# Three fused layers on one core: a recast second mixer, weight slots of twice the size, gate sums on VectorE

## The chip, the cores and the metric

One core of a Trainium2 chip runs one program: TensorE (PE), VectorE (DVE), ScalarE (ACT), GpSimdE (POOL) and SyncE (SP), each with its own instruction stream, joined by semaphores. The metric is the device time of one execution in microseconds, as the median of several. Everything is fp32; one fp32 matmul shows in the trace as two instructions, a transpose by matmul as one.

## The reference

A sequence of 256 tokens of width 1024 goes through two blocks. The first has two layers, each a mixer and an expert-choice mixture of experts (16 experts, 32 tokens each, width 1024); the second has one layer with a four-part mixer and a top-2 mixture of 16 experts of width 512. Each half layer is modulated by shift, scale and gate vectors, which are a vector times a large weight ("ada"). Shortened:

```python
cond = silu(c)
for l in range(2):                                   # first block
    shift, scale, gate = adaln(cond, ada_w[l, 0], ada_b[l, 0])        # 1024 x 3072
    h = rms_norm(x, mix_norm_g[l]) * (1 + scale) + shift
    y = fourier_conv_mixer(h) if l % 2 == 0 else windowed_attention(h)
    x = x + gate * y
    shift, scale, gate = adaln(cond, ada_w[l, 1], ada_b[l, 1])
    h = rms_norm(x, ffn_norm_g[l]) * (1 + scale) + shift
    x = x + gate * ec_moe(h)
x = rms_norm(x, final_norm_g)
# second block: ada_w_2 gives six vectors, for x and for the context ctx
hl, hc = modulated(rmsnorm(x)), modulated(rmsnorm(ctx))
u = hl @ w_in                                        # split into four parts of 256 columns each for:
a = diff_attention(...)          # 4 heads, 2 x 32 columns: softmax(q0 k0) - lam * softmax(q1 k1), then a norm per head
b = neighbourhood_attention(...) # 4 heads of 64, bias from a table
p = pool_mix(...); y = hyena_mix(...)                # y: two long convolutions by DFT matmuls
x = x + g1 * (concat(a, b, p, y) @ w_out)
x = x + g2 * moe(modulated(rmsnorm(x)))              # softmax router, best group of 4, top 2 in it
return rmsnorm(x, final_g)
```

## The kernel before, in words

All weights come from HBM once, in the order of a hand-written list (`order`), through a ring of `RING` = 14 slots of 1 MB in SBUF. `Stream.pump` issues the next transfer on SP's queue as soon as a slot is free; a slot is free when its user calls `st.done`. A transfer is [128 partitions x 8 KB]. The order is: constants and layer 0's `ada00`, `fc`, `ada01`, `fo`, then layer 0's 16 experts (three weights of 4 MB each), layer 1's attention weights and `ada`, its experts, the second block's `wi`, `ada20`, constants, `ada21`, `wo` (`w_out`), and its experts (w1, w3, w2 of 2 MB each).

`ada_steps` makes the vectors. "s" is the shift and scale half (16 pieces of 1024 columns), "g" the gate (8). With a letter in `ON_V`, VectorE adds the weight's rows, scaled by `cond`, into one tile (`add_rows`: L490 and L492, 128x1024 each), and TensorE only sums over partitions (L497); without it TensorE does all of the sums (L512, L555). These steps are fillers: the program calls `fill(n)` where an engine would wait. `weave` takes steps of several generators in turn, so that attention, projections (L1325, L1337), hyena, pooling and fillers stand between each other.

An expert-choice layer (`moe_ec`) first finds the norm of x, scales rows (`scale_rows`: L648 on VectorE, L649 on ScalarE), transposes (`plain_t`, L681), gets logits (L957, L963) and a softmax, picks each expert's tokens, gathers them by one-hot matmuls (L989) and runs the experts (L1052). Weighted rows go back by L1093, and in the last group x, its sum of squares and, after layer 1, the product with the final gain and its squares follow for each of four quarters (L1094, L614, L1099).

The second mixer (L1379 and on) norms twice, transposes (L659), projects (L1395, L1337, L1325), turns q and k (L1373) and then weaves. Attention A goes in 8 steps of one head: two score matmuls of 32 rows (L1436), reductions (L1442), exp (L1447), combination with lambda (L1452), four turns (L1419) and their copy (L1421), values (L1423, 4 matmuls of 64 columns). Its output is then normed and transposed again (`after_a`, L1373 on `oa`), and so is attention B's (L1373 on `va`). `wo` is L697. The last experts take tokens by top 2: `sc` are the softmaxed logits, L1689 to L1700 pick for one row block after the other, `keys` and `job` serve an extra run of a crowded expert, which is chosen at run time, `pair` gathers (L1743) for two experts, L1772 and L1797 are their matmuls.

On each engine instructions run in the order in which a scheduler of the framework put them; it starts from the order of the code and moves what is ready. The engines otherwise wait for semaphores alone.

## Time and profile before

| | |
|---|---|
| median of 3 runs | 1782.59 us (1780.39 to 1788.25) |
| profiled execution | 1785.29 us, of which the span is 1783.1 us |
| TensorE busy | 1421.8 us (80%), mean granted clock 0.857 |
| VectorE / ScalarE busy | 455.2 us (26%) / 242.9 us (14%) |
| moved by DMA | 635.93 MB, 357 GB/s on average |

The stages by TensorE's lines: mixer 0 to about 155 us, border of layer 0 to 184, its experts to 643, layer 1's attention to 775, its border and experts to 1272, the second mixer to 1468, the border to the last experts to 1498, these to 1763, the final norm and the output to the end. PE's share of busy time is an average over stages with different limits, so each stage is read by itself. The last 2 us between span and time lie around the span.

### The profile page before, as it was taken

The numbers are of one execution on the slowest core, as the hardware profiler recorded it, in microseconds if no ns is written. First come the engines' busy times: TensorE is split into PE (matmuls) and PEld (weight loads), VectorE is DVE, ScalarE is ACT, GpSimd is POOL, SyncE is SP. The second block draws the span as 40 slices with busy tenths as digits, with TensorE's granted clock in tenths as the row PEclk, the third lists the DMA queues.
The fourth block names the chain that finished last, engine by engine and source line by source line (L and its number), as shares of the span: only waits on it lengthen the run. The fifth ranks groups of instructions, "written<-read, shape, count | busy, mean of one in ns | idle before, by whom it ended". The sixth has DMA issues, their size and how long they took to land. (4 is left out here: it accounts for less than half of the span.)

```text
span 1783.1 us, 24944 instructions
## 1 busy us (share of the span) xinstructions
PE 1421.8 (80%) x10776; PEld 720.3 (40%) x10776; DVE 455.2 (26%) x1042; ACT 242.9 (14%) x556; POOL 10.7 (1%) x19
## 2 busy tenths in 40 slices
PE   6997877867666679987676776678799998999996
PEld 2444423323222234543232232235477745655453
DVE  2523212401010038541110100100333424333223
ACT  3021100100000012420200000000222312101012
POOL 0000000000000000000000000000000000000000
PEclk9997868878676689998787767868898998999998
DMA  9978899999999999289999999999931566999970
GB/s 375 421 310 325 346 420 421 420 421 421 420 422 421 420 410 408 101 354 420 421 420 421 421 420 421 421 421 420 409 107 51 206 242 239 421 421 415 392 297 25
DMA packets 89746, 635.93 MB, mean 357 GB/s; under 512 B 10944, under 2 KB 11072, under 8 KB 13344
## 3 DMA queue, kind: packets, MB, share of 16 engines
q1 hardware_dynamic: 87392, 630.67, 86.6%
q0 software_dynamic: 1952, 3.09, 0.5%
q8 instruction: 87, 1.43, 0.3%
q10 hardware_dynamic: 288, 0.52, 0.1%
q14 instruction: 27, 0.22, 0.0%
HBM read 633.25 MB, written 1.05 MB: 356 GB/s over the span
## 5 line engine op out<-in xcount | busy, mean ns | idle before, releaser
L1052 PE MATMUL b<-w,xg 128*32 128x256 f32 x4096 | 359.3, 493 | 172.6 <-DMA w<-in_moe_w_up_dram 99.8
L1052 PEld LDWEIGHTS b<-w,xg 128*32 128x32 f32 x4096 | 135.9, 132 | 392.7 <-DMA w<-in_moe_w_up_dram 150.2
L1052 PE MATMUL b<-w,hidT 128*32 128x256 f32 x2048 | 173.8, 476 | 71.5 <-DMA w<-in_moe_w_down_dram 55.3
L1072 DVE TENSOR_TENSOR hid<-b,sg 128x256 f32<-128x256 f32 x32 | 13.6, 425 | 499.0 <-PE b L1052 406.6
L1052 PEld LDWEIGHTS b<-w,hidT 128*32 128x32 f32 x2048 | 64.8, 130 | 166.6 <-DMA w<-in_moe_w_down_dram 95.3
L1772 PE MATMUL u<-w,xg 128*64 128x256 f32 x1088 | 128.0, 383 | 0.0
L1080 DVE SCALAR_TENSOR_TENSOR Y<-b,cc,gq 32x256 f32<-32x256 f32 x128 | 61.5, 481 | 224.2 <-PE b L1052 222.6
L1772 PEld LDWEIGHTS u<-w,xg 128*64 128x64 f32 x1088 | 78.2, 137 | 46.1 <-issue 10.3
L1797 PE MATMUL b<-w,hidT 128*64 128x512 f32 x272 | 65.8, 598 | 6.0 <-ACT hidT L1789 6.0
L1067 ACT ACTIVATE sg<-b 128x256 f32<-128x256 f32 x32 | 12.3, 383 | 424.7 <-PE b L1052 424.7
L697 PE MATMUL b<-w,n 128*128 128x512 f32 x128 | 56.0, 594 | 0.0
L1077 ACT COPY hidT<-b 128x256 f32<-128x256 f32 x32 | 11.9, 372 | 312.2 <-PE b L1075 312.2
L490 DVE SCALAR_TENSOR_TENSOR w<-w,cond 128x1024 f32<-128x1024 f32 x42 | 52.4, 1276 | 1.3 <-DMA w<-in_ada01s_dram 1.2
L1743 PE MATMUL b<-oh,n 128*128 128x128 f32 (+1 forms) x288 | 40.8, 301 | 3.5 <-DVE oh L1737 2.1
L1093 PE MATMUL b<-Y,gT 128*128 128x512 f32 x64 | 35.7, 702 | 9.5 <-DVE Y L1080 9.5
L1174 PE MATMUL b<-w,hT 128*128 128x512 f32 x96 | 43.1, 605 | 0.0
L1743 PEld LDWEIGHTS b<-oh,n 128*128 128x128 f32 x288 | 38.0, 212 | 11.3 <-issue 7.9
L822 PE MATMUL b<-w,hT 128*128 128x512 f32 x96 | 41.6, 593 | 1.1 <-DVE hT L671 1.1
L989 PE MATMUL b<-oh,n 128*128 128x128 f32 x256 | 39.9, 323 | 0.9 <-DVE oh L1032 0.9
L989 PEld LDWEIGHTS b<-oh,n 128*128 128x128 f32 x256 | 37.3, 233 | 7.2 <-issue 5.7
L1325 PE MATMUL b<-pe,w 128*128 128x256 f32 x160 | 38.6, 396 | 0.0
L1802 DVE TENSOR_TENSOR Y<-b,hkb 64x512 f32<-64x512 f32 x34 | 23.4, 688 | 53.6 <-PE b L1797 53.3
(439 smaller groups left out, 1383.9 us busy)
## 6 DMA issues: line engine op xcount, KB each, us to landing
w<-in_moe_w_gate_dram SPq DMA_DIRECT2D x128, 1024.0 KB, 19.8
w<-in_moe_w_up_dram SPq DMA_DIRECT2D x128, 1024.0 KB, 19.8
w<-in_moe_w_down_dram SPq DMA_DIRECT2D x128, 1024.0 KB, 19.8
w<-in_moe_w_dram SPq DMA_DIRECT2D x102, 1024.0 KB, 10.4
w<-in_wi_dram SPq DMA_DIRECT2D x10, 1024.0 KB, 19.8
w<-in_ada00s_dram SPq DMA_DIRECT2D x8, 1024.0 KB, 18.5
w<-in_ada01s_dram SPq DMA_DIRECT2D x8, 1024.0 KB, 20.6
w<-in_ada10s_dram SPq DMA_DIRECT2D x8, 1024.0 KB, 7.0
```

The source lines that it names most:

```text
L490: V.scalar_tensor_tensor(into[:, hs], w[:, hs], c, into[:, hs], op0=OP.mult, op1=OP.add)
L697: T.matmul(acc, mixT[:, kt, b * 128:(b + 1) * 128], w(kt)[:, h * 512:(h + 1) * 512], start=kt == first, stop=kt == last)
L822: T.matmul(p, hT[:, kt, b * 128:(b + 1) * 128], w(kt), start=kt == 0, stop=kt == 7)
L989: T.matmul(p[:, j * 128:(j + 1) * 128], n[:, b, dt * 128:(dt + 1) * 128], oh[:, b, g * 128:(g + 1) * 128], start=b == 0, stop=b == 1)
L1052: T.matmul(p[32 * q:32 * q + 32, :256], lhs(kt), w[:, k, q * 256:(q + 1) * 256], start=kt == 0, stop=kt == 7)
L1080: V.scalar_tensor_tensor(Y[32 * j:32 * j + 32, q * 256:(q + 1) * 256], pd[32 * q:32 * q + 32, :256], cc[32 * q:32 * q + 32, e:e + 1], gq[3 ...
L1093: T.matmul(p, gT[:, b * 128:(b + 1) * 128], Y[:, h * 512:(h + 1) * 512], start=True, stop=True)
L1174: T.matmul(p, hT[:, kt, b * 128:(b + 1) * 128], w(kt), start=kt == 0, stop=kt == 7)
L1325: T.matmul(p[:, j * 256:(j + 1) * 256], w(kt)[:, c0 + j * 128:c0 + (j + 1) * 128], h[:, kt], start=kt == 0, stop=kt == 7)
L1743: T.matmul(p[:, j * 128:j * 128 + m], n[:, b, dt * 128:(dt + 1) * 128], oh[:, b, :m], start=b == 0, stop=b == 1)
L1772: T.matmul(p[rows[h], :256], xg[:, kt, c], w[kt // 4][:, kt % 4, h * 256:(h + 1) * 256], start=kt == 0, stop=kt == 7)
L1797: T.matmul(pd[rows[h]], hidT[:, kt % 2, rows[kt // 2]], w[kt // 2][:, kt % 2, h * 512:(h + 1) * 512], start=kt == 0, stop=kt == 3)
```

## The change

It has seven parts. (1) `RING` becomes 7 with slots of 2 MB: the weights are laid out in HBM so that one transfer is [128 x 16 KB] and brings two of the former pieces; a slot frees when both are used, and a small constant takes a whole slot. (2) `ON_V`: the gates of (0,0) and (2,0) and all of (2,1) move to VectorE; in the second block these additions may stand only behind the last modulation or behind the first pair's one-hots (`queue_behind`). (3) The routers take x unnormalised and multiply the logits by r, and the rows are scaled after them; layer 1's last sums go to n first. (4) Both score copies of a step in layer 1's attention go to ScalarE. (5) The second mixer: one root of four columns, attention A in four steps of two heads with four score matmuls, values transposed in pairs of column tiles, no turns of the attentions' outputs, and reciprocals spread by matmuls. (6) In the last router both row blocks are picked by the same operations, and the first pair is gathered before the rest of the gate and the keys. (7) A job loads three transfers of 2 MB.

The core of the diff:

```diff
-ON_V = {(0, 0): "", (0, 1): "s", (1, 0): "g", (1, 1): "sg", (2, 0): "", (2, 1): ""}
-RING = 14
+ON_V = {(0, 0): "g", (0, 1): "s", (1, 0): "g", (1, 1): "sg", (2, 0): "g", (2, 1): "sg"}
+RING = 7
...
     def pump(self):
...
+            keys, shapes, ap = self.order[self.issued]
+            t = self.pool.tile([128, 2 * SLOT], F32, name="w")
+            self.nc.sync.dma_start(t[:, :ap.shape[1]], ap)
...
         def add_rows(kt, w, into):
+            with ExitStack() as behind:
+                if queue_behind:
+                    behind.enter_context(tc.issue_after(queue_behind[-1].ins))
+                add_rows_(kt, w, into)
...
-            scale_rows(n, x, rstd(ss))
-            fill(2)
             nT = [wk.tile([128, 8, 128], F32, name="xg", bufs=2) for _ in range(2)]
-            plain_t(nT, n)
+            plain_t(nT, x)
+            r = rstd(ss)
...
-            router(nT, rw, rbias, lg)
+            fill(2)
+            router(nT, rw, rbias, lg, r)
+            scale_rows(n, x, r)
...
+                        t = n[:, b, hs]
+                        V.tensor_tensor(t, x[:, b, hs], p, op=OP.add)
+                        A.activation(bank(), t, AF.Square, accum_out=ss[:, b, h:h + 1])
+                        V.tensor_tensor(x[:, b, hs], t, fg[:, h], op=OP.mult)
+                        sums(last, b, h, x)
...
-                    if u:
-                        A.copy(eT, p)
-                    else:
-                        V.tensor_copy(eT, p)
+                    A.copy(eT, p)
...
+            rs = inv_root(ms, 4)
+            r1, r2 = rs[:, 0:2], rs[:, 2:4]
             scale_rows(n, x, r2)
-            modulate(hT, turn(n), ada[2, 0])
+            queue_behind.append(modulate(hT, turn(n), ada[2, 0]))
             scale_rows(x, x, r1)
-            fill_until(lambda: ((2, 0), "g", 3) in st.freed)
...
+            def attend(po, es, vals, qb, j):
+
+                ets = [turned(e) for e in es]
+                at = j * 256 + qb * 128
                 for kb in range(4):
-                    T.matmul(po[:, h * 64:(h + 1) * 64], eT[:, kb * 128:(kb + 1) * 128], vals[:, kb, h * 64:(h + 1) * 64],
-                             start=kb == 0, stop=kb == 3)
+                    for u in range(2):
+                        h = 2 * j + u
+                        T.matmul(po[64 * u:64 * u + 64, at:at + 128], vals[:, kb, h * 64:(h + 1) * 64],
+                                 ets[u][:, kb * 128:(kb + 1) * 128], start=kb == 0, stop=kb == 3)
...
+                def scores(qb, j):
+                    pp = [bank() for _ in range(4)]
+                    for i in range(4):
+                        T.matmul(pp[i], qT[32 * i:32 * i + 32, j, qb * 128:(qb + 1) * 128], kT[32 * i:32 * i + 32, j], start=True, stop=True)
                     return pp
...
+            fill_until(lambda: (2, 0) in gqs and ((2, 0), "g", 0) in st.freed)
+            weave(hyena(), attention_b(), after_a(), chain(pooling(), filling(1, (2, 1))))
...
+            ts = {0: pair(0)}
+            queue_behind.append(ts[0]["last"])
+            fill(99)
```

What the scheduler makes of it, at three places. First TensorE in the second mixer, from the turns of q and k on. Before (L1373 turns, L1436 scores, L1325 projections, L1419 turns of the exponentials, L1423 values; x counts matmuls):

```order
L1373 MATMUL b<-cst,pe 128x128 x8
L1436 MATMUL b<-kT,qT 128x512 x4
L1325 MATMUL b<-pe,w 128x256 x8
L1419 MATMUL b<-cst,pe 128x128 x4
L1325 MATMUL b<-pe,w 128x256 x2
L1423 MATMUL b<-va,pe 128x64 x4
L1436 MATMUL b<-kT,qT 128x512 x2
L1325 MATMUL b<-pe,w 128x256 x6
L1419 MATMUL b<-cst,pe 128x128 x4
L1436 MATMUL b<-kT,qT 128x512
L1423 MATMUL b<-va,pe 128x64 x4
```

and after, where L1387, L1467, L1339 and L1351, L1432 and L1444 are the same in turn:

```order
L1387 MATMUL b<-cst,pe 128x128 x8
L1467 MATMUL b<-kT,qT 128x512 x4
L1339 MATMUL b<-pe,w 128x256 x16
L1351 MATMUL b<-w,pe 128x256 x16
L1432 MATMUL b<-cst,pe 128x128 x8
L1444 MATMUL b<-pe,va 64x128
L1467 MATMUL b<-kT,qT 128x512
L1444 MATMUL b<-pe,va 64x128 x7
L1467 MATMUL b<-kT,qT 128x512 x3
L1339 MATMUL b<-pe,w 128x256 x24
L1432 MATMUL b<-cst,pe 128x128 x8
L1467 MATMUL b<-kT,qT 128x512
```

The scores of the first step stand together, and those of the second stand as one among the eight value matmuls of the first step and three behind them; the third step begins in the same way. A step now has eight turns and eight value matmuls of 64x128.

Second TensorE at the border to the last experts. Before (L697 wo, L555 the gate's sums for `ada21g`, L681 transposes, L942 to L963 the router, L1702 the first rank sum):

```order
L697 MATMUL b<-w,n 128x512 x32
L555 MATMUL b<-w,cond 64x512 x6
L681 MATMUL b<-cst,n 128x128 x16
L942 MATMUL b<-vec,shsc_7693 128x16 x8
L957 MATMUL b<-xg,sg 32x128 x16
L555 MATMUL b<-w,cond 64x512
L963 MATMUL b<-cst,parts 128x16 x2
L555 MATMUL b<-w,cond 64x512 x9
L1702 MATMUL b<-one,cst 128x16
```

and after (L707 wo, L691 transposes, L952 to L973 the router, L1736 to L1740 the rank sums, L1777 and L1792 gather and scatter matrices, L1807 the first expert, L506 the gate's sum over partitions):

```order
L952 MATMUL b<-vec,shsc_7123 128x16 x8
L967 MATMUL b<-xg,sg 32x128 x16
L973 MATMUL b<-cst,parts 128x16 x2
L1736 MATMUL b<-one,cst 128x16
L1737 MATMUL b<-one,cst 128x16
L1738 MATMUL b<-one,cst 128x16
L1739 MATMUL b<-one,cst 128x16
L1740 MATMUL b<-one,cst 128x16
L1777 MATMUL b<-oh,n 128x128 x16
L1792 MATMUL b<-cst,ohg 128x128 x2
L1807 MATMUL u<-w,xg 64x256 x33
L506 MATMUL b<-w,cst 64x512 x2
```

The three groups of L555 are gone from the border, and one group of two L506 stands behind the first 33 matmuls of the experts.

Third VectorE at the same border, behind the ranks, after the change (L1892 keys, L1771 and L1788 one-hots, L501 and L499 `add_rows` of `ada21g`, L1784 the copies of gathered tokens, L1893 and L1894 the job's choice):

```order
L1892 SCALAR_TENSOR_TENSOR keys<-cnt,cst 128x16
L1771 TENSOR_SCALAR oh<-cst,rank 128x64 x4
L1788 TENSOR_SCALAR ohg<-cst,rank,gates 128x64 x4
L501 TENSOR_SCALAR w<-w,cond 128x1024
L1892 SCALAR_TENSOR_TENSOR keys<-cnt,cst 128x16 x2
L499 SCALAR_TENSOR_TENSOR w<-w,cond 128x1024
L1784 TENSOR_SCALAR xg<-b,shsc_7123 128x128
L499 SCALAR_TENSOR_TENSOR w<-w,cond 128x1024
L1784 TENSOR_SCALAR xg<-b,shsc_7123 128x128 x2
L499 SCALAR_TENSOR_TENSOR w<-w,cond 128x1024
L1784 TENSOR_SCALAR xg<-b,shsc_7123 128x128
L499 SCALAR_TENSOR_TENSOR w<-w,cond 128x1024
```

Each copy of gathered tokens has an addition of 1024 columns ahead of it.

## Rows read from the trace of the kernel before

**Rows 1.** view by windows: us; busy PE, PEld, DVE, ACT, POOL; clock; DMA.

```profile
184.00:643.00 459.00, 321.93 (x3265) 127.71 (x3258) 72.84 (x146) 27.98 (x59) 0.00 (x0) 0.77 1.01 419
...
790.00:1272.00 482.00, 344.15 (x3416) 159.10 (x3416) 61.97 (x135) 34.88 (x77) 0.58 (x1) 0.77 1.01 421
...
1316.00:1441.00 125.00, 121.21 (x626) 86.28 (x623) 48.75 (x112) 38.41 (x88) 1.59 (x3) 0.96 0.41 144
...
1472.00:1498.00 26.00, 19.30 (x134) 14.77 (x136) 14.81 (x83) 5.10 (x12) 0.00 (x0) 0.80 0.46 174
...
1498.00:1763.00 265.00, 252.93 (x1714) 143.32 (x1710) 74.52 (x173) 33.80 (x81) 0.00 (x0) 0.99 0.86 349
```

**Rows 2.** page, costliest groups: out<-in, shapes, xcount, then busy us, mean ns, idle before.

```profile
L1052 PE MATMUL b<-w,xg 128*32 128x256 f32 x4096 | 359.3, 493 | 172.6 <-DMA w<-in_moe_w_up_dram 99.8
...
L490 DVE SCALAR_TENSOR_TENSOR w<-w,cond 128x1024 f32<-128x1024 f32 x42 | 52.4, 1276 | 1.3 <-DMA w<-in_ada01s_dram 1.2
```

**Rows 3.** DMA view of 250:640, queue row: packets, MB, share of 16 engines.

```profile
q1 hardware_dynamic: 22485, 163.74, 101.0%
```

**Rows 4.** DMA view of 1770:1783 (the output's rows of 2 KB), queue row.

```profile
q10 hardware_dynamic: 288, 0.52, 10.7%
```

**Rows 5.** page, DMA queue row of the instruction queue.

```profile
q8 instruction: 87, 1.43, 0.3%
```

**Rows 6.** groups by line, PE, 0:160: the column sums of layer 0's two gates.

```profile
L555 PE MATMUL b<-w,cond 128*32 128x256 f32 x128 | 8.3, 383 | 0.0
```

**Rows 7.** timeline, PE, border of layer 0: start us, us, group, idle before.

```profile
157.09 2.79 PE L681 MATMUL b<-cst,n 128*128 128x128 f32 x16 [1.20 <-DVE n L648]
```

**Rows 8.** waits of PE, 643:790: us in total, times, longest us.

```profile
PE b L1234 <- DVE eT L1230: 4.9, 3, 2.2
```

**Rows 9.** timeline, DVE, start of the second mixer.

```profile
1274.21 0.69 DVE L1099 TENSOR_TENSOR x<-x,oh 128x512 f32<-128x512 f32 x1 [0.80 <-ACT b L614]
...
1276.35 0.69 DVE L1099 TENSOR_TENSOR x<-x,oh 128x512 f32<-128x512 f32 x1 [0.85 <-ACT b L614]
...
1280.53 0.75 DVE L648 TENSOR_SCALAR n<-x,root 128x1024 f32<-128x1024 f32 x1
```

**Rows 10.** timeline, PE, start of the second mixer.

```profile
1281.42 1.51 PE L659 MATMUL b<-cst,n 128*128 128x128 f32 x6 [4.57 <-DVE n L648]
1282.87 1.83 PE L555 MATMUL b<-w,cond_both 128*32 128x256 f32 x16
...
1285.78 13.98 PE L1395 MATMUL b<-w,pe 128*128 128x256 f32 x64
```

**Rows 11.** groups by line, PE, 1315:1389.

```profile
L1325 PE MATMUL b<-pe,w 128*128 128x256 f32 x128 | 31.5, 401 | 0.0
...
L1436 PE MATMUL b<-kT,qT 32*128 32x512 f32 x32 | 13.3, 702 | 0.8 <-ACT kT L1374 0.8
```

**Rows 12.** timeline, PE, attention A: four scores together, values of one head.

```profile
1315.22 1.14 PE L1436 MATMUL b<-kT,qT 32*128 32x512 f32 x8 [0.78 <-ACT kT L1374]
...
1328.46 1.10 PE L1423 MATMUL b<-va,pe 128*128 128x64 f32 x8
```

**Rows 13.** timeline, PE, layer 1's attention: 64-column pairs of 256 and 128 columns.

```profile
700.44 1.08 PE L1234 MATMUL b<-eT,v 128*64 128x256 f32 x8
...
707.18 0.66 PE L1249 MATMUL b<-cst,den 128*64 128x128 f32 x8
```

**Rows 14.** timeline, PE, 1388:1441: one piece of ada21s's sums.

```profile
1404.04 1.06 PE L512 MATMUL b<-w,cond 128*32 128x512 f32 x8
```

**Rows 15.** timeline, PE, border to the second block's experts.

```profile
1472.44 1.94 PE L681 MATMUL b<-cst,n 128*128 128x128 f32 x16 [1.90 <-DVE n L648]
...
1491.79 5.86 PE L1743 MATMUL b<-oh,n 128*128 128x128 f32 x32 [1.44 <-DVE jobat L1816]
```

**Rows 16.** timeline, DVE, the same border.

```profile
1483.11 0.69 DVE L563 TENSOR_TENSOR hkb<-b,hkb 128x512 f32<-128x512 f32 x1 [2.02 <-PE b L555]
...
1488.60 0.23 DVE L1700 SCALAR_TENSOR_TENSOR one<-cst,tif,et 128x16 f32<-128x16 f32 x1
```

More of the change, by code (lines that the diff above doesn't have):

```diff
@@ L394, in trunk_kernel, with put @@
     order = []
-    def put(key, ap):
-        order.append((key, ap))
+    def put(ap, *keys):
+        if len(keys) == 1:
+            order.append((keys, [ap.shape[1:]], ap))
+        else:
+            order.append((keys, [ap.shape[2:]] * 2, ap.rearrange("p i a b -> p (i a b)")))
     def ada_slots(key, parts="sg", rows=range(8)):
@@ L440, in trunk_kernel @@
     ada_slots((1, 0), "s")
[L441 to L442 removed]
+    put(I["flfw"], ("fl", 0), ("fw", 0))
     experts(0)
@@ L1466, in attention_a @@
[L1466 to L1469 removed]
+                    den = small.tile([128, 4], F32, name="den2")
+                    e = []
+                    for i in range(4):
+                        e.append(temp())
+                        A.activation(e[i], pp[i], AF.Exp, scale=32 ** -0.5, bias=nm[:, i:i + 1], accum_out=den[:, i:i + 1])
+                    d = den.rearrange("p (u c) -> p c u", c=2)
@@ new lines, in softmax @@
+                    V.tensor_copy(den0[:, qb, 2 * j:2 * j + 2], d[:, 0])
+                    cf = small.tile([128, 2], F32, name="cf")
+                    V.reciprocal(cf, d[:, 1])
+                    V.scalar_tensor_tensor(cf, cf, lam, d[:, 0], op0=OP.mult, op1=OP.mult)
+                    for u in range(2):
+                        V.scalar_tensor_tensor(e[2 * u], e[2 * u + 1], cf[:, u:u + 1], e[2 * u], op0=OP.mult, op1=OP.add)
+                    es[qb, j] = e[0::2]
+                for t in range(4):
+                    softmax(scores(*steps[t]), *steps[t])
@@ L1470, in attention_a @@
                     yield
-                    values(*steps[t])
-                    if t < 7:
-                        softmax(pp, *steps[t + 1])
+                    attend(po, es.pop(steps[t]), va, *steps[t])
+                A.copy(oa, po)
                 yield
@@ L1530, in attention_b @@
                     yield
-                    values(*steps[t])
+                    attend(po, es.pop(steps[t]), bv, *steps[t])
                     if t < 3:
@@ L1865, in pair @@
                 t = tiles()
-                take([(rank[:, :, e], gates[:, :, e]) for e in (e0, e0 + 1)], t)
+                t["last"] = take([(rank[:, :, e], gates[:, :, e]) for e in (e0, e0 + 1)], t)
                 return t
```

327 lines of the change are left out of this document (150 added, 177 removed).

## The prediction

> **What bounds it now.** I read the view by windows first, because the limit changes along the way. In both expert-choice stages, 184 to 643 and 790 to 1272, the DMA engines are busy all the time (share 1.01, 419 to 421 GB/s, [rows 1]) while TensorE is busy 322 of 459 and 344 of 482 us, at a granted clock of 0.77; the costliest group of the page agrees, since TensorE's idle time ahead of L1052 ends with a DMA [rows 2]. These 941 us are transfer. From 1316 on it is TensorE: busy 121.2 of 125 us in the second mixer and 252.9 of 265 in the last experts, where the DMA share falls to 0.41 and 0.86. In between lie borders in which short vector operations and norms hold TensorE: at 1472 to 1498 it is busy 19.3 of 26 us. So what the change takes from TensorE counts in full after 1272 (up to the experts); before, it counts only as far as it makes a layer's experts start sooner with their 14 MB waiting.
>
> **The change, part by part.** The sum is made against the profiled execution (1785.3 us), which lies 2.7 us, 0.15%, above the median; I do not carry that difference over, since it is below what a measurement tells (0.5%, about 9 us).
>
> *Slots of 2 MB.* The bytes stay. Each packet grows from 8 to 16 KB. In 250 to 640 the queue's 163.74 MB are 19,988 packets of 8 KB, and 101.0% of 16 engines for 390 us is 6302 us, so 315 ns each [rows 3]; the output's 256 packets of 2 KB take 10.7% of 16 x 13 us, so 87 ns each [rows 4]. A line through both is 38 ns per KB and 11 ns fixed. By it two packets of 8 KB cost 631 ns and one of 16 KB 620, 1.7% less: -16 us on 941. The other bound is 0 (the rate is that of the engines whatever the packet). I take the middle, **-8**, since the 2 KB row is of writes. The Trainium skill ("DMA: Bandwidth & Descriptors", section Bandwidth) lists 341 GB/s for 1 MB and 425 for 16 MB against a ceiling of 435. The trace does not agree for queued transfers: 1 MB pieces already give 421 here, and by that page's ceiling the most would be an estimated -30.
>
> A slot of two halves is free only when both are used. TensorE needs 359.3/256 = 1.4 us for 1 MB [rows 2], so at the start of a layer's experts, with the ring full, the first transfer starts 1.4 us later, and at the end the last 2 MB land as one: 0.5 to 1.4 more. Two layers: **+3.8** (+1 to +6).
>
> *Layer 0's gate sums on VectorE.* Half of L555's 8.3 us goes [rows 6], 0.6 comes back for the sums over partitions: -3.5 on TensorE. But eight additions of 0.75 to 1.28 us [rows 2], 9.7 us together, now stand on VectorE ahead of mixer 0's layer norm, which the transposes of z wait for. I take **-1**, between -3.5 and +6 (all in the way).
>
> *Borders of layers 0 and 1.* The transposes no longer wait for the normalised rows (1.20 us, [rows 7]): **-2.5** for two, -5 to +2, since vector work ahead of their copies remains.
>
> *Layer 1's score copies on ScalarE.* TensorE waits 4.9 us in all for VectorE's score copies there [rows 8]. ScalarE has the time: **-3.5**, -5 to +1 (both copies of a pair now queue on one engine).
>
> *Start of the second mixer.* Before, multiplication, square and addition follow each other at a pitch of 2.14 us from 1274.21 to 1276.35 [rows 9], because the product overwrites x, which ScalarE still squares. With the sum in n the pitch is that of two squares of about 0.8: -2.1 over four. One root of four columns instead of two after each other: -1. L555 (1.83 us) leaves the transposes [rows 10], in part hidden: -1.1. **-4.2**, -5.5 to -1. Transposes and projections follow unchanged.
>
> *Second mixer, first scores to wo* (125 us, TensorE 121). Scores: four matmuls of 32 rows together take 1.14 [rows 12]; all 16 (32 instructions) take 13.3 [rows 11], so the other twelve about 1.01 each. After, the order splits three of four steps 1 + 3 around the values: 1.14 + 3 x 2.15 = 7.6: -5.7. Values: 16 heads at 1.10 [rows 12] become 8 pairs; eight pieces of 64 x 256 side by side take 1.08 and of 64 x 128 0.66 [rows 13], so sixteen of 64 x 128 take 1.1 to 1.3: 17.6 to 9.6, -8. The eight turns of oa and va go (1.6). ada21s' sums: eight pieces of at least 1.06 [rows 14]: -8.5. Back come the spreading of the reciprocals (two times 1.3), the "half" sums and two sums over partitions (2.4): +5. TensorE: -18.8. Against that, VectorE gets 8 additions of ada20g and 16 of ada21s, 29 us beside its 48.8 in these 125 us, and they stand between parts of a softmax: reductions, exp, combination, turn, copy. I give 2.8 us to waits: **-16**, -24 to +1 (the last: rival 1).
>
> *Border to the last experts.* TensorE starts its turns 1.9 us plus part of 2.8 of L555 earlier (-3.4; it waits for n at 1472.44, [rows 15]). VectorE stood 2.02 us waiting for L555's last sums before routing went on [rows 16]: gone, -2.5. Routing, 1483.8 to 1488.8, takes 17 operations for both blocks instead of 24: -1.5. The key operations leave the one-hots: -0.4. Against it, ada21g's eight additions stand between the xg copies, and its sum over partitions among the first expert's matmuls: +3. **-5**, -8 to +3.
>
> *Last experts.* The same instructions; TensorE is the bound: seventeen runs (one is the run-time job) in 265 us [rows 1] are 15.6 each, and 6.29 MB at 421 GB/s are 14.9. **0**; a transfer up to 4% slower changes nothing there.
>
> Sum: -8 + 3.8 - 1 - 2.5 - 3.5 - 4.2 - 16 - 5 = -36.4, so **1749 us**.
>
> **Rivals.** 1: *VectorE or the clock eats the second mixer.* If more than half of the 29 us of additions delays a softmax for which TensorE then waits, the 16 us are gone and the mixer keeps its 125: 1765. For it: a step must wait for its four banks, and ada21s' first 2 MB land about when step two's combination stands behind them. Against it: L1325's 31.5 us of projections in the attention [rows 11] wait for no addition and can stand in the gaps. The same loss could come by the clock: where TensorE is busy 74%, at 1472 to 1498 [rows 1], the granted clock is 0.80, partly its lower level of 1.2 GHz, after waits; 0.96 while it is 97% busy. 100 us of work at 0.80 in place of 0.96 are +20: 1769, which I take into the same case. The Trainium skill ("TensorE: Matmul & The Clock Gate", section HAM oscillation) says that idle stretches between bursts put the array back to its lower clock; the rows agree, and the rule speaks against a mixer with less TensorE work per wait.
>
> 2: *Large packets pay in full.* -16 to -22 instead of -8, with wait-free additions: 1737. For it: the DMA is the bound for 941 us. Against: only one row of smaller packets.
>
> 3: *Large packets are slower.* The instruction queue's packets are 16.4 KB (87 for 1.43 MB), and 0.3% of 16 engines is 0.98 us each [rows 5], where two of 8 KB take 0.63. If the weights' rate falls by 5%, the 941 us grow by 47 and the last experts (15.7 us each, then above TensorE's 15.6) by 2: 1749 + 8 + 49 = 1806. From 3% the gain is gone, from 4% it is slower. Against it: these packets may come from elsewhere.
>
> That the change does not do what it says: the order shows each edit in place but for the four scores at once, which is in the sum.
>
> **How the numbers follow.** Forecast 0.63, rival 1 0.19, rival 2 0.12, rival 3 0.06. The likeliest case alone spans 1738 to 1762 by the terms' own bounds. For 8 in 10 I leave out rival 3, the far ends of rivals 1 and 2: 1733 to 1771. Faster by over 0.5% is below 1773.7: the forecast (0.63), rival 2 (0.12) and two thirds of rival 1 (0.12), so 0.87; the same: the rest of rival 1, 0.07; slower 0.06.
>
> **What would show it.** In the profile after: expert stages shorter by 3 to 5 us each with the rate at 423 to 427 GB/s (a rate of 421 says the term is 0, 410 rival 3); the score copies' wait gone; the projections of L1395 4 us sooner after layer 1's last L1093; first scores to wo in 106 to 112 us with TensorE above 92% busy and its clock above 0.93 (rival 1: 120 or more, waits for "pe" or "nm" of VectorE); from wo to the last experts 5 us less; experts to the end unchanged. Wrong would make it a wait at a layer's first expert that grows with the 2 MB pieces.

## The result, and the profile after

The changed kernel takes 1742.24 us in the median of 4 runs (1740.17 to 1744.46), against 1781.71 for the kernel before in the same comparison: a ratio of 0.977, 95% interval 0.974 to 0.980. The prediction said 1749, and 1733 to 1771 as its range. The profiled execution took 1742.27 us, with a span of 1740.5; by the two profiled spans the gain is 42.6 us. From the page after (the span, and what the DMA engines moved in each of 40 slices of it):

```profile
span 1740.5 us, 24033 instructions
...
GB/s 378 413 314 365 363 428 428 427 427 427 428 427 428 427 415 340 160 271 427 428 427 427 427 427 427 428 427 428 427 158 90 297 249 221 427 427 427 421 310 26
```

In the slices that lie within the expert stages the rate is now 427 to 428 GB/s; the page before has 420 to 422 in such slices. The view by windows, by the stages after (columns as in [rows 1]; the five lines answer its five):

```profile
177.00:633.00 456.00, 286.40 (x3265) 138.85 (x3261) 72.67 (x146) 27.91 (x59) 0.00 (x0) 0.84 1.00 424
...
790.00:1254.00 464.00, 299.94 (x3374) 157.54 (x3373) 56.39 (x122) 31.86 (x69) 0.58 (x1) 0.84 1.01 427
...
1298.00:1403.00 105.00, 100.35 (x613) 77.10 (x614) 61.38 (x116) 41.34 (x92) 1.59 (x3) 0.98 0.52 201
...
1430.00:1453.00 23.00, 14.49 (x115) 13.07 (x115) 16.15 (x71) 7.00 (x15) 0.00 (x0) 0.70 0.25 92
1453.00:1720.00 267.00, 250.16 (x1716) 143.21 (x1712) 83.54 (x198) 33.50 (x81) 0.00 (x0) 0.99 0.86 362
```

In the second mixer TensorE is busy 100.4 of 105 us where it was 121.2 of 125; in the border 14.5 of 23 us where it was 19.3 of 26; in the last experts 250 of 267 where it was 253 of 265.

The time between milestones of TensorE, in us, from one profiled execution of each kernel (an expert stage begins with the first matmul of the expert loop and ends with the last write back):

| stage | before | after | change | forecast |
|---|---|---|---|---|
| mixer 0, to the end of its wo | 152.4 | 151.0 | -1.4 | -1 |
| border to layer 0's experts | 31.3 | 25.8 | -5.5 | -1.25 |
| layer 0's experts | 464.3 | 459.7 | -4.6 | -2.1 |
| layer 1's mixer, to the end of its wo | 119.9 | 120.8 | +0.9 | -3.5 |
| border to layer 1's experts | 31.0 | 33.1 | +2.1 | -1.25 |
| layer 1's experts | 473.4 | 467.2 | -6.2 | -2.1 |
| to the second mixer's first scores | 42.9 | 40.4 | -2.5 | -4.2 |
| first scores to wo | 125.0 | 104.7 | -20.3 | -16 |
| wo and border to the last experts | 57.6 | 50.0 | -7.6 | -5 |
| last experts, first to last up matmul | 264.0 | 266.6 | +2.6 | 0 |

The end behind it is the same within 0.3 us. The sum is -42.5 us where -36.4 were forecast; the single stages miss by more, in both directions: six by 18 us on the good side, four by 12 on the bad one. By the medians the gain is 39.5 us: the profiled execution of the kernel before, at 1785.3 us, lies 3.6 above its median. A second profile of the kernel before (`before_again` below) agrees with the first within 0.6 us in all but two stages: layer 1's experts took 469.7 us and the stretch to the first scores 44.8, so these two changes are uncertain by 3.7 and 1.9 us.

The transfers, in a stretch of layer 0's experts (DMA view of 250 to 600 after, the row that answers [rows 3]: packets, MB, share of 16 engines; 1134 of the packets are of a few bytes):

```profile
q1 hardware_dynamic: 10242, 149.23, 100.3%
```

That is 100.3% of 16 x 350 us for 9108 packets of 16 KB, 617 ns each, where a line through the rows of before gave 620.

The second mixer by TensorE's groups, 1298 to 1403 (columns as in [rows 11]):

```profile
L1432 PE MATMUL b<-cst,pe 128*128 128x128 f32 x64 | 8.6, 274 | 2.5 <-DVE pe L1486 2.4
L1467 PE MATMUL b<-kT,qT 32*128 32x512 f32 x32 | 7.9, 640 | 0.8 <-ACT kT L1388 0.8
...
L1444 PE MATMUL b<-pe,va 128*64 128x128 f32 x64 | 6.4, 318 | 0.3 <-ACT pe L1434 0.3
L1444 PE MATMUL b<-pe,bv 128*64 128x128 f32 x64 | 6.1, 282 | 0.5 <-ACT pe L1434 0.5
```

Scores fell from 13.3 to 7.9 us (forecast 7.6). The values (L1444) take 12.5 us in two groups. The longest wait, 2.4 us, is for the combination on VectorE (L1486). A wait for the combination stood there before too, 2.2 us in two parts (waits of TensorE before, 1316 to 1441: total, times, longest):

```profile
PE b L1419 <- DVE pe L1452: 2.2, 2, 1.4
```

The border to the last experts (timeline of TensorE, answers [rows 15]):

```profile
1402.78 27.63 PE L707 MATMUL b<-w,n 128*128 128x512 f32 x64
1430.25 1.47 PE L691 MATMUL b<-cst,x 128*128 128x128 f32 x12
...
1443.63 0.58 PE L1736 MATMUL b<-one,cst 128*128 128x16 f32 x2 [5.90 <-DVE one L1734]
...
1447.02 5.62 PE L1777 MATMUL b<-oh,n 128*128 128x128 f32 x32 [1.10 <-DVE oh L1771]
```

The transposes follow wo at once, where before they came 4.6 us behind its end and waited for n ([rows 15]); the largest idle time left, 5.9 us, is the choice of experts on VectorE.

### The profile page after: what moved, and what is told of

Same layout as the page of the kernel before. It is cut to its first block, busy times and chain, and to the rows that moved or that the text cites. A ratio compares the mean times of both kernels' runs of the same rounds, so it can differ in the third digit from the quotient of the medians.

```text
span 1740.5 us, 24033 instructions
## 1 busy us (share of the span) xinstructions
PE 1313.8 (75%) x10612; PEld 723.0 (42%) x10612; DVE 487.8 (28%) x1051; ACT 249.4 (14%) x567; POOL 10.7 (1%) x19
## 5 line engine op out<-in xcount | busy, mean ns | idle before, releaser
L1065 PE MATMUL b<-w,xg 128*32 128x256 f32 x4096 | 316.6, 465 | 219.4 <-DMA w<-in_moe_w_up_dram 134.6
L1065 PEld LDWEIGHTS b<-w,xg 128*32 128x32 f32 x4096 | 148.9, 129 | 385.0 <-issue 137.7
L1065 PE MATMUL b<-w,hidT 128*32 128x256 f32 x2048 | 160.7, 467 | 83.2 <-DMA w<-in_moe_w_down_dram 77.7
L1065 PEld LDWEIGHTS b<-w,hidT 128*32 128x32 f32 x2048 | 76.4, 129 | 154.5 <-DMA w<-in_moe_w_down_dram 62.3
L1807 PE MATMUL u<-w,xg 128*64 128x256 f32 x1088 | 125.0, 384 | 0.0
L499 DVE SCALAR_TENSOR_TENSOR w<-w,cond 128x1024 f32<-128x1024 f32 x77 | 97.0, 1280 | 4.9 <-DMA w<-in_ada21s_dram 3.2
L1807 PEld LDWEIGHTS u<-w,xg 128*64 128x64 f32 x1088 | 78.3, 138 | 47.5 <-issue 11.7
L1832 PE MATMUL b<-w,hidT 128*64 128x512 f32 x272 | 63.2, 598 | 9.8 <-ACT hidT L1824 9.8
L707 PE MATMUL b<-w,n 128*128 128x512 f32 x128 | 56.0, 594 | 0.0
L1777 PE MATMUL b<-oh,n 128*128 128x128 f32 (+1 forms) x288 | 39.3, 297 | 3.2 <-DVE oh L1771 3.2
L1777 PEld LDWEIGHTS b<-oh,n 128*128 128x128 f32 x288 | 36.8, 209 | 9.2 <-issue 6.3
L1000 PE MATMUL b<-oh,n 128*128 128x128 f32 x256 | 35.6, 305 | 0.9 <-DVE oh L1045 0.9
L1832 PEld LDWEIGHTS b<-w,hidT 128*64 128x64 f32 x272 | 18.6, 136 | 42.2 <-issue 28.3
L707 PEld LDWEIGHTS b<-w,n 128*128 128x128 f32 x128 | 24.0, 190 | 28.8 <-issue 28.7
## 6 DMA issues: line engine op xcount, KB each, us to landing
w<-in_moe_w_up_dram SPq DMA_DIRECT2D x64, 2048.0 KB, 30.9
w<-in_moe_w_down_dram SPq DMA_DIRECT2D x64, 2048.0 KB, 30.9
w<-in_ada10s_dram SPq DMA_DIRECT2D x4, 2048.0 KB, 11.5
```

The lines of the kernel that those rows point to most:

```text
L499: V.scalar_tensor_tensor(into[:, hs], w[:, hs], c, into[:, hs], op0=OP.mult, op1=OP.add)
L707: T.matmul(acc, mixT[:, kt, b * 128:(b + 1) * 128], w(kt)[:, h * 512:(h + 1) * 512], start=kt == first, stop=kt == last)
L1000: T.matmul(p[:, j * 128:(j + 1) * 128], n[:, b, dt * 128:(dt + 1) * 128], oh[:, b, g * 128:(g + 1) * 128], start=b == 0, stop=b == 1)
L1065: T.matmul(p[32 * q:32 * q + 32, :256], lhs(kt), w[:, k, q * 256:(q + 1) * 256], start=kt == 0, stop=kt == 7)
L1777: T.matmul(p[:, j * 128:j * 128 + m], n[:, b, dt * 128:(dt + 1) * 128], oh[:, b, :m], start=b == 0, stop=b == 1)
L1807: T.matmul(p[rows[h], :256], xg[:, kt, c], w[kt // 4][:, kt % 4, h * 256:(h + 1) * 256], start=kt == 0, stop=kt == 7)
```

## The experiments

Each starts from the changed kernel, unless it says otherwise. "Mixer", "border" and "experts" are the stages of the table above.

### What the packet and the slot are worth

`two_loads` fills a slot by two transfers, `half_parts` by two of 64 partitions, `four_loads` by four, and `own_slots` gives each piece of 1 MB its own slot again:

```diff
 # two_loads (four_loads: step SLOT // 2)
-            self.nc.sync.dma_start(t[:, :ap.shape[1]], ap)
+            for c in range(0, ap.shape[1], SLOT):
+                c1 = min(c + SLOT, ap.shape[1])
+                self.nc.sync.dma_start(t[:, c:c1], ap[:, c:c1])
 # half_parts
-            self.nc.sync.dma_start(t[:, :ap.shape[1]], ap)
+            for c in (0, 64):
+                self.nc.sync.dma_start(t[c:c + 64, :ap.shape[1]], ap[c:c + 64])
 # own_slots
-RING = 7
+RING = 14
...
-            t = self.pool.tile([128, 2 * SLOT], F32, name="w")
+            t = self.pool.tile([128, SLOT], F32, name="w")
             self.nc.sync.dma_start(t[:, :ap.shape[1]], ap)
...
```

> The changed kernel, but each 2 MB slot is filled by two transfers of 1 MB with rows of 8 KB; the slots stay as they are. Theory A (the rate follows the packet: 315 ns for 8 KB, 617 ns for 16 KB in the two profiles): the rate in the expert stages falls back from 427 to 421 GB/s, each of the two stages of about 460 us becomes 6 to 7 us longer, less 1 us at its end because half a slot lands earlier; 1753 us in all (1750 to 1756). Rival B (the packet does not matter, the gain comes from half as many slots and waits): rate stays at 427, 1742 us.

> The changed kernel, but each slot is filled by two transfers of 1 MB, each of 64 partitions with rows of 16 KB. Theory A (the packet counts): rate 427 GB/s as in the changed kernel, 1742 us (1739 to 1746). Rival C (the size of a transfer counts, by a fixed cost of each): rate 421 as with two transfers of 8 KB rows, 1753 us.

> The changed kernel, but each slot is filled by four transfers of 512 KB with rows of 4 KB. Theory A by the line through 315 and 617 ns (14 ns fixed, 37.7 per KB): 165 ns a packet, 3 to 4% below the rate of 8 KB packets, about 400 to 408 GB/s: 1785 us (1775 to 1800). Rival B: rate 427, 1742 us.

> The changed kernel with 14 slots of 1 MB, each with its own transfer of 8 KB rows and its own freeing, as before the change; all else stays. Theory A with a price for the large slot (first refill 0.9 us later, last 2 MB of a layer 2.5 us longer, per layer): the rate is 421 as with two transfers, but the two expert stages win back 5 to 7 us together against that run: 1748 us (1745 to 1751). Rival D (the large slot costs nothing): the same time as with two transfers, 1753 us.

Measured: 1756.5 us with two loads (ratio to the kernel before 0.984, 0.982 to 0.986), 1793.5 with four (1.005, 1.003 to 1.006), 1748.5 with own slots (0.980, 0.977 to 0.983), and 2812.1 (2713.8 to 2819.8) with half the partitions. Two loads lie 0.5 us above the range that was expected; where the difference comes from is said below. The DMA rows of 250 to 600, two loads, four loads, half the partitions:

```profile
q1 hardware_dynamic: 20179, 146.96, 101.0%
```

```profile
q1 hardware_dynamic: 39215, 142.79, 102.4%
```

```profile
q1 hardware_dynamic: 5777, 75.73, 100.9%
```

Without the few-byte packets (2241, 4359, 1155) these are 315 ns for a packet of 8 KB, 165 ns for 4 KB and 1222 ns for 16 KB into half the partitions, and by the MB over 350 us 420, 408 and 216 GB/s, where one load has 426. The three sizes into 128 partitions lie on one line: 37.7 ns per KB and 13.7 ns fixed. That is theory A, by its number: 165 ns was expected for 4 KB. Whether the fixed part belongs to the packet or to the transfer is not told by these runs. A transfer into 128 partitions always has 128 packets of data, and the few-byte packets come one to every eight of them at each size (1134 to 9108, 2241 to 17938, 4359 to 34856), so a cost of about 110 ns for each few-byte packet would give the same three numbers. The run meant to part the two (`half_parts`) showed another limit: the engines are busy all the time (100.9%), and each packet takes twice as long. So rival C (a cost of each transfer) is not excluded.

By stages, the experts of layers 0 and 1 took 466.6 and 474.1 us with two loads, 6.9 more each than with one: the packet. With own slots they took 464.4 and 472.5, 2.2 and 1.6 less than with two loads: the price of freeing 2 MB at a time. For layer 0 the profiles of runs with one transfer of 2 MB agree within 0.7 us, so the 2.2 stands clear of that; for layer 1 they differ by 2.6 us, so the 1.6 does not. Theory A's 1748 us for own slots came out at 1748.5, but not by its parts: it expected 5 to 7 us from the two expert stages, which gave 3.8, and the rest came from layer 1's border (29.9 us against 32.7, by the clock, see below) and from the last experts (269.8 against 272.6).

The last experts took 272.6 us with two loads and 266.6 with one, though TensorE waited for a weight 0.6 us in all there. The matmuls are the same 1717 instructions, in another order, and TensorE is busy with them 258.5 us instead of 250.4, and 267.5 with four loads (granted clock 0.98 in both, 0.99 with one). That was not expected by any theory; it led to `in_order` below.

### Which engine adds

```diff
-ON_V = {(0, 0): "g", (0, 1): "s", (1, 0): "g", (1, 1): "sg", (2, 0): "g", (2, 1): "sg"}
+ON_V = {(0, 0): "", (0, 1): "s", (1, 0): "g", (1, 1): "sg", (2, 0): "", (2, 1): ""}
```

> The changed kernel with ON_V as before the change: the gate sums of layer 0's mixer and all of the second block's ada sums are TensorE's again; all else stays. Theory A (in the second mixer TensorE is the bound, so its 12 to 14 us of sums come back in full, and 24 additions on VectorE were covered): first scores to wo 104.7 becomes 115 to 118 us; mixer 0 and its border 1 to 2 us longer; the last gate's sums stand between the gather and the first expert, +5, while the first experts lose VectorE's additions, -2; in all 1757 us (1752 to 1761). Rival E (the additions stand in the softmax chain and cost about what they save): first scores to wo 104 to 107, 1744 us.

1759.5 us (ratio 0.987, 0.984 to 0.989). First scores to wo took 113.3 us, 8.6 more than after. The groups that came back (TensorE, 1290 to 1425):

```profile
L521 PE MATMUL b<-w,cond 128*32 128x512 f32 x64 | 12.5, 603 | 0.0
...
L564 PE MATMUL b<-w,cond_both 128*32 128x256 f32 x64 | 4.9, 385 | 0.0
```

17.4 us of sums came back for 8.6 of time: TensorE's idle time there fell from 4.6 to 0.7 us, the wait for the combination with it, values and spreading ran in less busy time (10.0 and 2.2 us instead of 12.5 and 3.1; the granted clock is 1.00 here and 0.98 after the change), and the sums over partitions are not needed. So theory A holds with less than it said, and rival E falls. The recast attention without the moved sums is then worth 125.0 - 113.3 = 11.7 us, the moved sums 8.6. Border and wo took 57.6 (+7.6): the last gate's 32 sums stand in one piece of 7.1 us (L564) between the gather and the first expert. The last experts took 263.3 (-3.3): whether the last gate's additions beside the experts cost these 3.3 us, or the order in which the blocks then come, is taken up at `in_order` below.

### Layer 1's score copies

```diff
-                    A.copy(eT, p)
+                    if u:
+                        A.copy(eT, p)
+                    else:
+                        V.tensor_copy(eT, p)
```

> The changed kernel with layer 1's score copies as before: one of each two on VectorE. Theory A (the wait for the copies was only moved: the pair of column tiles runs side by side only when both copies are there, 1.08 us for eight matmuls before and 1.57 after): layer 1's mixer 120.8 us stays within 1.5, total 1742 (1740 to 1745). Rival F (the prediction's term): +3.5, 1746 us.

1741.2 us (0.977, 0.975 to 0.979); layer 1's mixer 120.7 us against 120.8. The value matmuls after, and in this run (groups of TensorE):

```profile
L1248 PE MATMUL b<-eT,v 128*64 128x256 f32 x64 | 12.4, 397 | 1.5 <-ACT eT L1244 1.5
```

```profile
L1251 PE MATMUL b<-eT,v 128*64 128x256 f32 x64 | 9.9, 391 | 5.3 <-DVE eT L1247 4.9 <-ACT eT L1245 0.3
```

One such group of eight, after and in this run (timeline of TensorE):

```profile
698.69 1.56 PE L1248 MATMUL b<-eT,v 128*64 128x256 f32 x8 [0.30 <-ACT eT L1244]
```

```profile
703.95 1.08 PE L1251 MATMUL b<-eT,v 128*64 128x256 f32 x8 [1.07 <-DVE eT L1247]
```

With both copies on ScalarE the wait is 1.5 us instead of 5.3 and the busy time 12.4 instead of 9.9. A group then starts when the first of its two copies is there, 0.30 us late instead of 1.07, but its pairs no longer all run side by side, and it takes 1.56 us instead of 1.08. Theory A is right, and the change's fourth part is worth nothing that can be measured.

### Transfers that land too late

```diff
-            self.nc.sync.dma_start(t[:, :ap.shape[1]], ap)
+            last = keys[0][0] == (2, 1) or keys[0][0][0] == "down" and keys[0][0][2] == E - 1
+            step = SLOT if last else 2 * SLOT
+            for c in range(0, ap.shape[1], step):
+                c1 = min(c + step, ap.shape[1])
+                self.nc.sync.dma_start(t[:, c:c1], ap[:, c:c1])
```

> The changed kernel, but the slots of ada21 and those of the last expert's down weights of layers 0 and 1 are filled by two transfers of 1 MB. Theory A (a 2 MB transfer lands too late in two places: the second mixer's additions wait for ada21s and hold up a softmax, 3.3 us; the last 2 MB of a layer, about 1 us each): first scores to wo 101.5, the experts of layers 0 and 1 458.5 and 466, total 1737 us (1735 to 1740). Rival I (those 3.3 us of the run with two transfers everywhere came from elsewhere): 1742 us.

1738.7 us (0.975, 0.973 to 0.977). First scores to wo took 101.4 us, 3.3 less, as with two loads everywhere (101.4) and own slots (100.5). The turns' wait, 2.5 us in the group L1432 above, is now:

```profile
L1436 PE MATMUL b<-cst,pe 128*128 128x128 f32 x64 | 8.6, 274 | 1.3 <-DVE pe L1490 1.3
```

So 2 MB of ada21s landing as one piece held up VectorE's additions and a softmax behind them. The wait is only half of the 3.3 us: TensorE's idle time in the stage falls from 4.6 to 3.0 us, and its busy time from 100.1 to 98.4, because the granted clock, 0.59 and 0.84 in the 6 us behind that wait in the profile after, is 1.00 through the whole stage here. The other half of the expectation fails: the experts of layers 0 and 1 took 459.8 and 469.5 us, not less than after. The longest wait for a down weight is 4.0 us in the profile after (waits of TensorE, 184 to 633: total, times, longest) and 2.9 with the smaller pieces at the very end, and yet the stage is no shorter.

```profile
PE b L1065 <- DMA w<-in_moe_w_down_dram: 39.7, 22, 4.0
```

### The order of the last experts

Each block of matmuls of the last experts gets an edge of issue order to the block ahead of it in the code:

```diff
+                            with behind(get is None):
+                                g = T.matmul(p[rows[h], :256], xg[:, kt, c], w[kt // 4][:, kt % 4, h * 256:(h + 1) * 256], start=kt == 0, stop=kt == 7)
+                        last_pe.append(g)
```

where `behind()` opens `tc.issue_after(last_pe[-1].ins)`; turns, down, scatter and gather are treated alike.

> The changed kernel with TensorE's blocks of the last experts held in the order of the code (up, turn of the expert before, second up, down of the expert before, scatter, gather), by edges of issue order alone. Theory G (the last experts are bound by TensorE, and their pace of 15.9 us comes from the order: interleaved groups switch between 64-column tiles and the whole array and leave the turn without cover; the first pairs of the kernel before ran in the code's order at 14.65 us each): first to last expert matmul 266.6 becomes 248 to 252 us, total 1725 us (1723 to 1729). Rival H (they are bound by the transfers, 14.7 us each at 427 GB/s with what the ring holds at the start): 1738 to 1742 us, with waits for w.

1729.4 us (1722.9 to 1730.7; ratio 0.971, 0.969 to 0.973), the last experts 248.1 us instead of 266.6. The profiled execution was the fastest of the four: the median is 12.8 us below the changed kernel's, where the profiled spans differ by 19.4, and it lies 0.4 us above theory G's range. After the change a second half of a pair looks like this (timeline of TensorE; L1807 up, L1777 gather, L1832 down, L1755 scatter):

```profile
1615.31 3.65 PE L1832 MATMUL b<-w,hidT 128*64 128x512 f32 x16 [0.52 <-ACT hidT L1824]
1618.89 3.70 PE L1755 MATMUL b<-Y,sT 128*128 128x512 f32 x8
1622.52 3.67 PE L1807 MATMUL u<-w,xg 128*64 128x256 f32 x32
1626.12 2.27 PE L1777 MATMUL b<-oh,n 128*128 128x128 f32 x18
1628.33 3.67 PE L1807 MATMUL u<-w,xg 128*64 128x256 f32 x32
1631.93 1.83 PE L1777 MATMUL b<-oh,n 128*128 128x128 f32 x14
```

and in this run (L1829 up, L1846 turn, L1859 down, L1769 scatter):

```profile
1570.14 3.60 PE L1859 MATMUL b<-w,hidT 128*64 128x512 f32 x16
1573.58 3.62 PE L1829 MATMUL u<-w,xg 128*64 128x256 f32 x32
1577.13 0.44 PE L1846 MATMUL b<-cst,hid 128*128 128x128 f32 x2
1577.50 3.67 PE L1829 MATMUL u<-w,xg 128*64 128x256 f32 x32
1581.00 3.60 PE L1859 MATMUL b<-w,hidT 128*64 128x512 f32 x16
1584.54 3.70 PE L1769 MATMUL b<-Y,sT 128*128 128x512 f32 x8
```

Ups of 32 instructions no longer have parts of the next gather between them, and the turn has an up on either side. The waits of the stretch, after the change (1452 to 1720) and in this run (1450 to 1710, so that the last 0.5 and 0.6 us of the run-time job are in it):

```profile
PE b L1832 <- ACT hidT L1824: 9.3, 14, 0.9
PE b L1822 <- DVE hid L1818: 4.1, 7, 0.6
```

```profile
PE u L1829 <- DMA w<-in_moe_w_dram: 1.4, 2, 0.8
PE b L1859 <- ACT hidT L1850: 1.0, 2, 0.5
PE b L1846 <- DVE hid L1841: 0.6, 1, 0.6
```

Up to the last up matmul, 13.4 us of waits for the expert's own intermediate results become 0.5, and a wait of 1.4 us for weights appears. Theory G holds, rival H does not: at 29.3 us for two experts TensorE's pace is now about that of the transfers (an estimated 29.5: 12.6 MB at 427 GB/s).

Idle time is 11.5 of the 18.5 us, and 7.0 are busy time. Of these, 3.3 are the clock at the run-time job at the end, whose gather and ups ran at the lower level after the change and at the higher one here. `copies_two` shows that they can do so without the edges: it has the changed kernel's matmuls of the last experts in the changed kernel's order, and its gather of the job took 3.79 us instead of 5.57, its ups 7.13 instead of 8.39, and its last experts 263.4 instead of 266.6. In this run gather and ups took 3.79 and 7.13 too. The job's gather after the change and in `copies_two` (timeline of TensorE):

```profile
1705.11 5.57 PE L1777 MATMUL b<-oh,n 128*128 128x64 f32 x32 [2.07 <-DVE oh L1771]
```

```profile
1705.41 3.79 PE L1780 MATMUL b<-oh,n 128*128 128x64 f32 x32 [2.07 <-DVE oh L1774]
```

So at the same clock the order is worth 15.3 us there. How the 3.7 us of busy time that are left divide between switches of column tiles and other things was not tried, nor whether the order keeps the clock up at the job, as in both profiles with it (this one and `best`).

### The borders and the clock

```diff
 # old_borders
-            plain_t(nT, x)
-            r = rstd(ss)
+            scale_rows(n, x, rstd(ss))
+            fill(2)
+            plain_t(nT, n)
...
-            fill(2)
-            router(nT, rw, rbias, lg, r)
-            scale_rows(n, x, r)
+            router(nT, rw, rbias, lg, None)
 # fill_first
+            if l:
+                fill(2)
             plain_t(nT, x)
...
-            fill(2)
+            if not l:
+                fill(2)
```

> The changed kernel with the routers of layers 0 and 1 as before the change: rows scaled first, fillers, then transposes of the scaled rows. Theory J (the first border got 5.5 us shorter mostly because without the wait for n, 1.2 us behind another of 1.0, TensorE keeps its full clock through transposes and router): with the wait back, mixer 0's wo to the first expert 25.8 becomes 29 to 31 us with the granted clock at half in the router; at the second border the sums stand ahead of the transposes again: 33.1 becomes 30 to 31. Total 1743 (1740 to 1746). Rival K (the clock has no part, only the wait itself): 27 and 34 us, 1744 in all, with the clock at 1.0 in both.

> The changed kernel with layer 1's filler (16 instructions of L521) traced ahead of the transposes in the border, as it stood before the change. Theory J: TensorE does work in place of idling behind the gate's row, the transposes run at full clock (1.97 us for 16 instead of 3.60), wo to the first expert 33.1 becomes 31, total 1740. Rival K (the 2 us come from the order of router and filler, not from the clock): 33 us.

`before_again` is the kernel before, without an edit, profiled once more:

> The kernel before, unchanged, profiled once more, for the clock at the two borders alone. Theory L (where the half-clock stretch falls is not set by the change, it shifts from execution to execution): mixer 0's wo to the first expert is 28 us with the transposes at 1.97 and the router at 1.86 and 1.08 us, or again 31 with 2.8, 3.4 and 1.9. Theory J (the kernel before always loses its clock there, by the wait for n): 31.3 again, and the same durations.

`old_borders` took 1744.0 us (0.978, 0.975 to 0.981), `fill_first` 1742.4 (0.977, 0.975 to 0.980), `before_again` 1785.2. First border: 27.1 us with the old order against 25.8 (25.8 to 26.5 in the other runs with the new one). The transposes and the router (L691, L952, L967 and their like) after, in `old_borders`, and in `before_again`:

```profile
154.41 1.91 PE L691 MATMUL b<-cst,x 128*128 128x128 f32 x16
156.15 1.86 PE L952 MATMUL b<-vec,shsc 128*128 128x16 f32 x16
157.94 1.08 PE L967 MATMUL b<-xg,sg 128*32 128x128 f32 x32
```

```profile
156.69 1.97 PE L691 MATMUL b<-cst,n 128*128 128x128 f32 x16 [1.20 <-DVE n L657]
158.50 1.86 PE L952 MATMUL b<-vec,shsc 128*128 128x16 f32 x16
```

```profile
157.28 2.78 PE L681 MATMUL b<-cst,n 128*128 128x128 f32 x16 [1.20 <-DVE n L648]
159.85 3.43 PE L942 MATMUL b<-vec,shsc 128*128 128x16 f32 x16
163.22 1.94 PE L957 MATMUL b<-xg,sg 128*32 128x128 f32 x32
```

The same 16 instructions of the router's bias (L952, L942) take 1.86 us at a granted clock of 1.00, the level of 2.4 GHz, and 3.43 at 0.50, that of 1.2. `old_borders` has the same waits ahead (1.02 and 1.20 us) as the kernel before and keeps the higher level. So theory J falls: the wait for n costs about 1 us by itself, and does not bring the lower clock. The kernel before had a low stretch (time at the lower clock) over transposes and router in both of its profiled executions. In the changed kernel it is not gone but comes later: read in slices of 2 us, the granted clock is 0.50 from 158 us on before and from 161 us on after, when transposes and router are done and TensorE mostly waits for VectorE. Why it comes later is open.

Second border: 33.1 us with the filler first as without, so theory J falls here too. At this border too the lower level stays where it is in time, and what stands in it is slow:

```profile
761.78 3.42 PE L521 MATMUL b<-w,cond_both 128*32 128x512 f32 x16
765.13 1.97 PE L691 MATMUL b<-cst,x 128*128 128x128 f32 x16
```

Here 16 sums take 3.42 us and the transposes 1.97; after, the transposes took 3.60 and the sums 1.92. In the kernel before the sums took 1.90 in the first profile and 3.36 in `before_again`, so at this border the clock differs between executions of one program, as theory L has it; at the first border the two profiles agree. In the runs with the transposes and sums at the higher level (`own_slots`, `copies_two`) the border took 29.9 and 30.9 us, in the others 32.7 to 33.2.

### Both gains together

`best` is `in_order` with two transfers for the slots of ada21 alone.

> The changed kernel with the last experts in the order of the code and ada21's slots filled by two transfers of 1 MB. If both gains stand beside each other (18.5 us in the last experts, 3.3 in the second mixer), 1720 us against the 1742 of the changed kernel (1716 to 1727). If the last experts then wait for their transfers (29.3 us for two experts on TensorE against 29.5 of transfer), 1727 to 1735, with waits for w.

1722.9 us (1720.4 to 1727.5, 5 runs), ratio 0.966, interval 0.964 to 0.969; the changed kernel's was 0.974 to 0.980. First scores to wo 101.5, last experts 248.2: in the stages the gains stand beside each other as expected, and the total is in the expected range. By the profiled spans 18.1 us are won against the changed kernel, where the two stages give 21.6; the other stages, mixer 0 above all (153.4 us against 151.0), take the rest. TensorE waits 1.6 us in all for weights in the last experts, so the transfers do not hold them up.

## Why the prediction was right

The result is in the range and near the likeliest case, and the three largest terms (the second mixer, the slots, the border to the last experts) came out by the mechanisms that were named, each larger than forecast. That the sum is so close is in part luck: one term gave nothing, a stage that was put at nothing moved, and the misses stand against each other, 18 us one way and 12 the other.

**Slots of 2 MB: mechanism right, size short.** The line gave -16 for both layers and I took -8; `two_loads` shows 6.9 per layer, -13.8. The step that failed was to halve what the line through two rows gave. The slot's price was +3.8, and `own_slots` shows 2.2 + 1.6 = 3.8, of which the 1.6 is within what layer 1's stage varies by. Rival 2 (large packets pay in full) was, for this term, the better case; rival 3 is gone, since large packets are faster. The Trainium skill ("DMA: Bandwidth & Descriptors", section Bandwidth) ties the rate to the size of a transfer; the runs have 408, 420 and 426 GB/s for 512 KB, 1 MB and 2 MB, far closer together than its 341 for 1 MB and 425 for 16 MB, and below its ceiling of 435.

**Layer 0's gate sums: -1, measured -1.4 for the mixer.** `sums_pe` puts it 3.9 us higher, so the sums' move is worth more than the term, but seven profiles with the same mixer 0 and the same slots ended it between 149.8 and 153.4 us, so the parts can't be told apart.

**Borders of layers 0 and 1: -2.5, measured -3.4, for the wrong reason.** The wait for n is worth about 1 in the first (`old_borders`), close to the 1.25 forecast; most of the rest of -5.5 is the clock's low stretch (3.3 us in transposes and router, 0.9 in the gather), and so is the +2.1 at the second, since `copies_two`, with its transposes at the higher level, took 30.9 us there against 31.0 before. The prediction had the clock in rival 1 alone, not in its borders.

**Score copies: -3.5, measured nothing.** The step that failed was to count TensorE's wait as time won. The wait stood ahead of matmuls that run side by side only when both copies are there; taking it away moved it into the group.

**Start of the second mixer: -4.2, measured -2.5.** The term itself was right. The pitch of the sums fell from 2.14 to 1.34 us (L1114, 1255.01 and 1256.35 on VectorE), and from the last write back to the first projection (L1395, now L1408) 13.5 us became 9.7, so -3.8. But the projections then began in the clock's low stretch:

```profile
1267.37 15.23 PE L1408 MATMUL b<-w,pe 128*128 128x256 f32 x64
```

They took 15.23 us instead of 13.98 [rows 10]. Before, L555's sums stood in that stretch (1.83 us for 16 that took 1.07 just ahead of it). In `copies_two`, where the stretch ends sooner, the projections took 13.98 again and the whole stage 38.8 us, which is -4.1. "Transposes and projections follow unchanged" is the step that left this out.

**First scores to wo: -16, measured -20.3.** TensorE's busy time fell by 20.9 us, close to the -18.8 of the term. The 2.8 us for waits were not needed: the wait for the combination is 2.4 us after and was 2.2 before, and TensorE's idle time in the stage rose from 3.8 to 4.6 only. `halves` shows that 3.3 us of what is left are the late landing of ada21s, half of it wait and half the lower clock behind it. Rival 1 (the additions or the clock eat the mixer) falls: TensorE is busy 96% there at a granted clock of 0.98. Values at 12.5 us were forecast as 9.6 (10.0 in `sums_pe`, at a clock of 1.00), sums at 8.5 were 12.5 of busy time.

**Border to the last experts: -5, measured -7.6**, by the steps that were named, with other sizes. TensorE starts its turns 4.8 us sooner behind wo (3.4 forecast); from the router's end to the first rank sum 2.1 us are won and from there to the gather 1.8 (4.4 forecast for both); transposes and router together take 1.3 us longer, which was not forecast. The 3 us for additions between the copies of gathered tokens did not come: the gather, up to the first expert, takes 5.8 us instead of 6.0.

**Last experts: 0, measured +2.6.** That TensorE is the bound was right, that it therefore does not change was wrong. `sums_pe` has 263.3 us, at the same low clock at the job (its gather and ups 14.6 us as after), so the 3.3 us between the two come with the moved sums: 1.3 are the sums over partitions that now stand among the experts (L506), and 1.9 are longer waits for the experts' own intermediate results. `in_order` has these sums too and takes 248.1, with those waits all but gone, so the order makes the waits, and VectorE's work does not force them. The prediction read 15.6 us an expert as TensorE's pace; with another order of the same matmuls it is 29.3 for two, and `in_order` wins 15.3 us there at the same clock.

## What to carry to other kernels

A wait that one instruction ends is not yet time won: ask which instructions behind it had to stand together, and read busy time and wait of that group as one number. Where an engine is the bound, compare the same work at several places of the profile: where the granted clock is the same, two paces for one loop say that the order, and not the work, sets the time. Look at the clock of a stretch before giving its time to an edit, and at a second execution before giving it a few microseconds. Larger transfers pay in a stream and cost by their landing; make them large in a stream and small where one consumer waits.

## What the runs showed of the hardware

With the queue full, packets of 4, 8 and 16 KB into 128 partitions took 165, 315 and 617 ns, so 408, 420 and 426 GB/s: 37.7 ns per KB and 13.7 ns fixed, whether of the packet or of the transfer. The same 16 KB packets into 64 partitions at a time take 1222 ns, 216 GB/s, with all engines shown busy. At the borders the granted clock falls to its lower level for some microseconds, at a place that can differ between executions of one program (the same 16 sums 1.90 us in the first profile before and 3.36 in `before_again`) and between runs with the same matmuls in the same order (the job's gather 5.57 us after, 3.79 in `copies_two`).
